# The first layer's start of a two-layer backbone: modulation, norm and first products in another order

## The chip, the cores and the metric

The kernel runs on one core of a Trainium2 chip. The metric is the time of one execution in microseconds (us) on the device. Five engines take their instructions in order, each from its own list, and wait for one another by semaphores: TensorE (PE, matrix products and transposes), VectorE (DVE), ScalarE (ACT), GpSimd (POOL) and SyncE (SP, which issues most loads).

## The reference

Two layers are run over 128 context tokens and 256 latent tokens (384 in all, of width 1024). What the change touches is the begin of layer 0:

```python
def rmsnorm(x, g):
    return x * rsqrt(mean(x * x, axis=-1) + EPS) * g
...
m = c @ w_ada + b_ada                      # shift, scale, gate of each of 1024 channels
h = rmsnorm(x, g1) * (1 + scale) + shift   # one set for context tokens, one for latent tokens
z = h @ w_in                               # split among four parallel groups:
# A neighbourhood attention, B a state-space (S5) block, C grouped-query attention, D latent attention
```

Group B is a diagonal complex recurrence. The kernel computes it by tables of powers of its complex decay factors (P), rotations (rw) and products of these with the input and output matrices B and C.

## The kernel before, in words

Activations stand transposed in SBUF, channels on the 128 partitions, 384 tokens along a row: x is eight such rows. Every matrix product of 32-bit numbers is done as three with rounded parts, high by high, low by high and high by low (L296, L297, L298). Each weight tile (`raw`) is therefore rounded by ScalarE (`hi`, L288), and VectorE subtracts to get the remainder (`lo`, L289); activations likewise have `ah` and `al`.

`first` (L1386 on) opens layer 0. It sums the squares of the eight rows of x (`prestat`), transposes the sums and makes the inverse norm (`inv_rms`). Then it goes over the eight rows k of 128 channels. `load(k)` issues on SyncE the two 512 KB tiles of modulation weights of the row, and every second row 512 KB of input weights; five modulation tiles fit at once (NA0). `mod(k)` is 16 matmuls (`pa`) and an eviction to `ar` on ScalarE. `norm(k)` transposes `ar` (L1428), reduces it on VectorE (L1431), adds the bias (`mods`, L1433), makes the gain (L1437), splits the weights, and for the context and the latent segment apart writes `ah` and `xn` on ScalarE (L1443, L1445) and `al` on VectorE (L1449). `products(k - LAG)` are the twelve matmuls of a row two rows back; `over_rms` (L1477) multiplies x by the inverse norm, five rows ahead of the loop and three after row 0.

Beside this VectorE computes group B's parameters: `fill(n)` takes n steps from a generator, first the parameters (`s5_params`, the s5t names; part of it on GpSimd: the powers P, and u and f), then the rotation `s5_rot` by doubling (`rw`, to 816 columns, L490 to L501) and the steps behind it. ScalarE copies the powers into the tables PQ and PF (L622 to L628) and the rotation into three buffers w (L662 on); a fourth, of magnitudes, is written by VectorE (L666). Four stores on GpSimd's queue (L672) write all to DRAM as `sw`. The buffers w stand in memory that the attention uses later (k4, v4, bias). Behind `first`, `tables0` (L1529) loads B, C and D and makes for each of four blocks of groups a table `eb` (512 columns, from PQ) and `ca` (640 columns, from PF); TensorE transposes `eb` (L707) and multiplies `ca` by the input factor (`ptr<-ca,bb`, L726).

The order of TensorE, ScalarE, VectorE and SyncE within `first` is that of the code, written by hand; GpSimd's and all that follows is ordered by a scheduler from priorities, and the mixer's parts by a list of steps.

Of the kernel before, what the change touches and what calls it, by code (L numbers as in the profile page):

```python
# [12 lines left out]
F32 = mybir.dt.float32  # L13
# [7 lines left out]
L = 2  # L21
# [17 lines left out]
NX = 5  # L39
FA = (4, 3, 4, 3, 4, 3, 4, 3)  # L40
FB = (8, 8, 4)
FK = ((0, 0, 0, 0, 0, 0), (1, 1, 1, 2, 2, 2), (1, 1, 1, 2, 2, 2), (1, 1, 1, 2, 2, 2), (1, 1, 1, 2, 2, 2), (1, 1, 1, 2, 2, 2), (1, 1, 1, 2, 2, 2), (1, 1, 1, 2, 2, 2))
FX = (6, 4, 4, 2, 2, 2, 2, 2)
MG = 0
WK = (0, 0, 0)
# [8 lines left out]
LAG = 2  # L54
# [74 lines left out]
def _prepare(a):  # L129
# [79 lines left out]
    r["cst"] = _constants()[0]  # L209
# [7 lines left out]
def _program(tc, I, O):  # L217
# [25 lines left out]
    def adjacent(calls):  # L243
# [6 lines left out]
    s5p = cp.tile([128, 5, 32], F32, name="s5p")  # L250
    A.dma_start(s5p, I["s5p"].rearrange("p (a b) -> p a b", a=5))
    csb = cp.tile([128, 8, 2], F32, name="csb")
    A.dma_start(csb, I["cT"].rearrange("p (k s) -> p k s", k=8))
    _, co = _constants()
    cst = cp.tile([128, int(co[-1])], F32, name="cst")
    A.dma_start(cst[:, :int(co[2])], I["cst"][:, :int(co[2])])
    ident, W1, W2, W4, RG, RM, cosg, sing, cosm, sinm, nadd = [
        cst[:, int(co[i]):int(co[i + 1])] for i in range(11)]
# [4 lines left out]
    vec = cp.tile([128, L * VPL], F32, name="vec")  # L263
    A.dma_start(vec[:, :VPL], I["vec"][:, :VPL])
# [3 lines left out]
    def vcol(l, i, n=1):  # L268
        return vec[:, l * VPL + i:l * VPL + i + n]
# [247 lines left out]

    def s5_params(qp, rest):
# [98 lines left out]
        G.tensor_tensor(f_[1], a[5], rden, op=OP.mult)  # L617
        yield

        def copies():  # L620
            for i, p in enumerate(P):
                A.activation(PQ[i][0:64], p[0:64, 0:8].rearrange("p t g -> p g t"), AF.Copy)  # L622
                yield
                A.activation(PQ[i][64:128], p[64:128, 7::-1].rearrange("p t g -> p g t"), AF.Copy)
                yield
                A.activation(PF[i][0:64, 0:9], p[0:64], AF.Copy)
                yield
                A.activation(PF[i][64:128, 1:10], p[64:128, ::-1], AF.Copy)  # L628
                yield
# [17 lines left out]
    def s5_rot(l, w, w4, qp, cmp):  # L647

        lg = slice(16 * l, 16 * l + 16)
        V.memset(w[0][:, :, 0:1], 1.0)  # L650
        V.memset(w[1][:, :, 0:1], 0.0)
        for i in range(2):
            V.tensor_copy(w[i][:, :, 1], u8[i][:, lg])
            yield
        h = 1
        while h < NC - 1:
            n = min(h, NC - 1 - h)
            shp = [128, 16, n]
# [3 lines left out]
        A.activation(w4[0], w[0], AF.Copy)  # L662
        A.activation(w4[1], w[1], AF.Copy)
        A.activation(w4[2], w[1], AF.Copy, scale=-1.0)
# [721 lines left out]
    def first(up, steps, rest):  # L1386
# [38 lines left out]
        def norm(k, ar, xb):  # L1425
            tr = pt()
            for q in range(2):
                PE.transpose(tr[:, 128 * q:128 * q + 128], ar[:, 128 * q:128 * q + 128], ident)  # L1428
            n = FK[k]
            m = tiny((2, 2))  # L1430
            V.tensor_reduce(m, tr[:, :256].rearrange("p (i c r) -> p i r c", i=2, c=4)[:, :, 0:2], axis=AX.X, op=OP.add)  # L1431
            fill(n[0])
            V.tensor_tensor(mods[0][:, k:k + 9:8], m,  # L1433
                            vcol(0, VO["adab"] + k, 9)[:, 0:9:8, None].to_broadcast([128, 2, 2]), op=OP.add)
            fill(n[1])
            Am = tiny((2,))
            V.tensor_scalar(Am, mods[0][:, 8 + k], 1.0, vcol(0, VO["n1"] + k), op0=OP.add, op1=OP.mult)  # L1437
            fill(n[2])
            W.append(split1(wr[k // 2], 512 * (k % 2), 512 * (k % 2) + 512))
            xn = kp.tile([128, XT[2]], F32, name="xn", tag=XT[0], bufs=XT[1])  # L1440
            hi, lo = act_pair()
            for s, (a, b) in enumerate(NSEG):
                A.activation(hi[:, a:b], xb[k // 2][:, k % 2, a:b], AF.Identity, scale=Am[:, s:s + 1],  # L1443
                             bias=mods[0][:, k, s:s + 1])
                A.activation(xn[:, a:b], xb[k // 2][:, k % 2, a:b], AF.Copy, scale=Am[:, s:s + 1])  # L1445
                late_a = nc.cur_bb.bb.instructions[-1]
            for s, (a, b) in enumerate(NSEG):
                fill(n[3 + s])
                V.scalar_tensor_tensor(lo[:, a:b], xn[:, a:b], mods[0][:, k, s:s + 1], hi[:, a:b].bitcast(F32),  # L1449
                                       op0=OP.add, op1=OP.subtract)  # L1450
            late = nc.cur_bb.bb.instructions[-1]
            fill(n[5])
            H.append((hi, lo))
            return late, late_a
# [19 lines left out]
        def over_rms(k):  # L1474
            if k % 2 == 0:
                xb.append(pools[1].tile([128, 2, T], F32, name="xb", tag="q3", bufs=NQ))
            V.tensor_tensor(xb[k // 2][:, k % 2], x[:, k], bc[:, :T], op=OP.mult)  # L1477

        for k in range(NX):
            over_rms(k)  # L1480
            fill(FX[k])
        for k in range(8 + LAG):
            if k < 6:
                load(k + 2)
            if k == 6:
                SY.dma_start(cst[:, int(co[2]):], I["cst"][:, int(co[2]):])
                SY.dma_start(vec[:, VPL:], I["vec"][:, VPL:])
            if 0 < k < 8:
                ars.append(mod(k))
            if k >= LAG:  # L1490
                products(k - LAG)
            if k < 8:
                late, late_a = norm(k, ars[k], xb)
            if k == 0:
                for i in range(NX, 8):
                    over_rms(i)
                    fill(FX[i])
                for _ in steps[0]:
                    pass
                steps[0] = itertools.chain(*rest)  # L1500
            for _ in range(WK[k] if k < LAG else 0):
                PE.matmul(zs[3][:, :T], warm[:, :128], warm, start=True, stop=True)
# [26 lines left out]
    def tables0():  # L1529
        bcd = s5_load(0, cmp)  # L1530
# [50 lines left out]
```

## Time and profile before

| | |
|---|---|
| median of 3 runs | 1104.14 us (1103.63 to 1106.66) |
| profiled run | 1105.24 us, span 1103.5 us, mean granted clock 0.987 |
| busy, TensorE | 1059.3 us, 96% of the span |
| busy, VectorE | 801.5 us, 73% |
| busy, ScalarE | 582.4 us, 53% |
| busy, GpSimd | 85.5 us, 8% |

The profile is of one execution. Busy time is a sum over the whole span; how full an engine is in one stage is seen from its busy time in that stretch. In rows of instructions the first number is the start in us from the span's start, the second the time that the row's instructions took.

### The profile page before, as it was taken

What the parts mean: (1) busy time and instruction counts of PE and PEld (TensorE: products, weight loads), DVE (VectorE), ACT (ScalarE), POOL (GpSimd) and SP (SyncE); (2) the same over time, 40 slices, a digit from 0 to 9 for tenths busy, and PEclk for the clock granted to TensorE, in tenths of its full rate; (3) what the DMA queues carried; (4) which work ended last, traced back from release to release, by engine and by line L of the source; (5) the groups of instructions that cost most, each with busy time, mean ns of one, the idle gap of its engine ahead of it and who ended that gap; (6) DMA issues with size and microseconds to landing.
All of it is one profiled execution on the core that took longest, in us unless ns stands there. A gap on an engine that the chain in (4) does not pass through costs nothing.

```text
span 1103.5 us, 18695 instructions
## 1 busy us (share of the span) xinstructions
PE 1059.3 (96%) x6724; PEld 904.8 (82%) x6724; DVE 801.5 (73%) x2026; ACT 582.4 (53%) x1251; POOL 85.5 (8%) x197
## 2 busy tenths in 40 slices
PE   6799988999999999999999999899999999999998
PEld 3577665447989999999999787545799999999998
DVE  6898677767899954679967787667669775476753
ACT  3754535455676543455457545564568553355532
POOL 4213111000100000001110220100000000000000
PEclk8999998999999999999999999999999999999999
DMA  8979866454554434445454874435333433433343
GB/s 331 320 260 304 246 207 225 156 179 172 172 178 134 140 106 139 131 134 163 129 158 157 218 233 137 129 125 183 116 115 96 138 114 117 148 126 123 116 131 98
DMA packets 64700, 182.19 MB, mean 165 GB/s; under 512 B 15840, under 2 KB 19168, under 8 KB 64608
## 3 DMA queue, kind: packets, MB, share of 16 engines
q1 hardware_dynamic: 55456, 152.52, 42.6%
q0 software_dynamic: 8576, 28.16, 8.3%
q8 instruction: 53, 0.87, 0.3%
q10 hardware_dynamic: 576, 0.32, 0.1%
q14 instruction: 39, 0.32, 0.1%
HBM read 166.19 MB, written 14.78 MB: 164 GB/s over the span
## 4 chain that ended last, share of the span: by engine, by line
PE 65%; DVE 4%; DMA 2%; ACT 1%; issue 0%; POOL 0%; SPq 0%; DVEq 0%; POOLq 0%; ACTq 0%
PE pz L296 11%; PE pz L297 10%; PE pz L298 10%; PE psc L298 8%; PE psc L297 8%; PE psc L296 8%; PE pa L319 2%; PE psc L959 1%; DVE lo L289 1%; DMA bias<-rpb 1%; PE ptr L963 1%; PE po L978 1%; DMA tbw<-sw 1%; PE psc L782 0%; DMA sw<-rw 0%
## 5 line engine op out<-in xcount | busy, mean ns | idle before, releaser
L288 ACT ACTIVATE hi<-raw 128x512 fp32r<-128x512 f32 (+2 forms) x396 | 228.1, 585 | 275.1 <-PE pz L297 109.1
L289 DVE TENSOR_TENSOR lo<-raw,hi 128x512 fp32r<-128x512 f32 (+2 forms) x396 | 250.2, 635 | 150.4 <-ACT hi L288 103.6
L296 PE MATMUL pz<-ah,hi 128*128 128x386 f32 (+1 forms) x616 | 213.8, 348 | 1.4 <-ACT gs L882 0.8
L297 PE MATMUL pz<-al,hi 128*128 128x386 f32 (+1 forms) x616 | 210.8, 343 | 1.0 <-DVE al L427 1.0
L298 PE MATMUL pz<-ah,lo 128*128 128x386 f32 (+1 forms) x616 | 210.2, 341 | 0.1
L296 PEld LDWEIGHTS pz<-ah,hi 128*128 128x128 f32 x616 | 116.5, 189 | 18.9 <-issue 13.4
L297 PEld LDWEIGHTS pz<-al,hi 128*128 128x128 f32 x616 | 117.0, 190 | 6.0 <-issue 3.6
L298 PEld LDWEIGHTS pz<-ah,lo 128*128 128x128 f32 x616 | 116.7, 190 | 3.0 <-issue 2.2
L296 PE MATMUL psc<-ah,hi 128*128 128x386 f32 (+1 forms) x336 | 114.2, 340 | 0.0
L298 PE MATMUL psc<-ah,lo 128*128 128x386 f32 (+1 forms) x336 | 113.9, 339 | 0.1
L297 PE MATMUL psc<-al,hi 128*128 128x386 f32 (+1 forms) x336 | 114.0, 339 | 0.0
L319 PE MATMUL pa<-raw,cw 128*32 128x256 f32 x640 | 62.5, 393 | 3.5 <-DMA raw<-ada 3.5
L296 PEld LDWEIGHTS psc<-ah,hi 128*128 128x128 f32 x336 | 63.5, 189 | 0.7 <-issue 0.4
L298 PEld LDWEIGHTS psc<-ah,lo 128*128 128x128 f32 x336 | 63.4, 189 | 0.4 <-DVE lo L289 0.4
L297 PEld LDWEIGHTS psc<-al,hi 128*128 128x128 f32 x336 | 63.7, 189 | 0.0
L296 PE MATMUL pz<-fh,hi 128*128 128x384 f32 x176 | 59.4, 338 | 0.1
L298 PE MATMUL pz<-fh,lo 128*128 128x384 f32 x176 | 59.5, 338 | 0.0
L297 PE MATMUL psc<-fl,hi 128*128 128x384 f32 x176 | 59.3, 337 | 0.0
L296 PE MATMUL psc<-fh,hi 128*128 128x384 f32 x176 | 59.3, 337 | 0.0
L297 PE MATMUL pz<-fl,hi 128*128 128x384 f32 x176 | 59.3, 337 | 0.0
L298 PE MATMUL psc<-fh,lo 128*128 128x384 f32 x176 | 59.3, 337 | 0.0
L936 ACT ACTIVATE P<-psc,ty 128x384 f32<-128x384 f32 (+1 forms) x56 | 32.2, 576 | 34.8 <-DVE ty L935 30.9
(431 smaller groups left out, 1950.3 us busy)
## 6 DMA issues: line engine op xcount, KB each, us to landing
raw<-wup SPq DMA_DIRECT2D x88, 512.0 KB, 3.5
raw<-ada SPq DMA_DIRECT2D x80, 512.0 KB, 4.6
raw<-win SPq DMA_DIRECT2D x30, 512.0 KB, 5.5
raw<-wdn SPq DMA_DIRECT2D x32, 384.0 KB, 3.1
raw<-wdn SPq DMA_DIRECT2D x32, 320.0 KB, 2.8
a<-ada SPq DMA_DIRECT2D x16, 512.0 KB, 6.1
raw<-wout SPq DMA_DIRECT2D x16, 512.0 KB, 3.5
se<-tbo POOLq DMA_DIRECT2D x16, 256.0 KB, 4.4
```

The lines of the kernel that those rows point to most:

```text
L288: A.activation(hi[:, :n], raw[:, a:b], AF.Copy)
L289: V.tensor_tensor(lo[:, :n], raw[:, a:b], hi[:, :n].bitcast(F32), op=OP.subtract)
L296: PE.matmul(out, wh, xh, start=start, stop=False)
L297: PE.matmul(out, wh, xl, start=False, stop=False)
L298: PE.matmul(out, wl, xh, start=False, stop=stop)
L319: PE.matmul(acc[32 * c:32 * c + 32, 256 * h:256 * h + 256], cw[:, kc], raw[:, 256 * c:256 * c + 256], start=kc == 0 and h == 0, stop=kc == ...
L936: A.activation(P[:, :w], S[:, :w], AF.Exp, bias=mx, scale=scale, accum_out=rs)
L959: PE.matmul(S[:, :T], qf(1 + qb), kf(128, 512), start=True, stop=True)
L963: PE.transpose(tr[:, 128 * kb:128 * kb + 128], P[:, 128 * kb:128 * kb + 128], ident)
L978: calls.append(lambda kb=kb, j=j: PE.matmul(o[64 * j:64 * j + 64, 128:T], heads[j][2](1 + kb), PTs[j][1][:, kb].rearrange("p q c -> p (q c ...
```

## The change

The loads of the state-space parameters, of c, of the first constants (the identity and a matrix of ones) and of layer 0's small vectors, four on ScalarE's queue, are one tensor `boot` with one load. The rest of the constants and layer 1's vectors are loaded at row 4, not at row 6. B, C and D of layer 0 are loaded behind the instruction that writes f (`mark`).

The rows are pipelined in another way. The transposes of row k+1 stand behind the products of row k-1 (one row back in place of two); the modulation runs two rows ahead, and its eviction stands ahead of the row's copies on ScalarE. Weights are rounded one row ahead. The inverse norm is copied from PSUM to SBUF once (`bcs`), and multiplied to x one row ahead. ScalarE writes the normed row in full precision (`y`, two segments) and then one rounded copy of 384 columns; VectorE subtracts them in one instruction. The fill steps per row (FK) are nine in six places before, and six (1, 1 and 4) in rows 2 to 7 after; what is left of the parameters comes behind row 0's remainder.

The eight copies into PQ and PF and, in layer 0, the three of the rotation go from ScalarE to GpSimd.

```diff
-FK = ((0, 0, 0, 0, 0, 0), (1, 1, 1, 2, 2, 2), ...)   # seven such rows
-FX = (6, 4, 4, 2, 2, 2, 2, 2)
+FK = ((0, 0, 0),) * 2 + ((1, 1, 4),) * 6
...
+    boot = cp.tile([128, nb + 160], F32, name="boot")
+    A.dma_start(boot, I["boot"])
...
         G.tensor_tensor(f_[1], a[5], rden, op=OP.mult)
+        mark.append(nc.cur_bb.bb.instructions[-1])
...
-                A.activation(PQ[i][0:64], p[0:64, 0:8].rearrange("p t g -> p g t"), AF.Copy)
+                G.tensor_copy(PQ[i][0:64], p[0:64, 0:8].rearrange("p t g -> p g t"))
...
+            G.tensor_copy(w4[0], w[0])
+            G.tensor_copy(w4[1], w[1])
+            G.tensor_scalar(w4[2], w[1], -1.0, None, op0=OP.mult)
...
+        def rows_hi(k, Am):
+            y = kp.tile([128, T], F32, name="y", tag="sq", bufs=5)
             hi, lo = act_pair()
             for s, (a, b) in enumerate(NSEG):
+                A.activation(y[:, a:b], xb[k // 2][:, k % 2, a:b], AF.Identity, scale=Am[:, s:s + 1],
                              bias=mods[0][:, k, s:s + 1])
+            A.activation(hi[:, :T], y[:, :T], AF.Copy)
...
+        def rows_lo(k, y):
+            V.tensor_tensor(lo[:, :T], y[:, :T], hi[:, :T].bitcast(F32), op=OP.subtract)
...
+        load(2)
+        tr = turned(0)
+        ars.append(mod(1))
+        weights_hi(0)
+        over_rms(0, bc)
+        for k in range(8):
+            if k + 3 < 8:
+                load(k + 3)
+            if k + 2 < 8:
+                ars.append(mod(k + 2))
+            Am = gain(k, tr)
+            y = rows_hi(k, Am)
+            if k == 0:
+                A.activation(bcs[:, :T], bc[:, :T], AF.Copy)
+            weights_lo(k)
+            if k < 7:
+                weights_hi(k + 1)
+                over_rms(k + 1, bcs)
+            rows_lo(k, y)
+            if k:
+                products(k - 1)
+            if k < 7:
+                tr = turned(k + 1)
+            if k == 0:
+                for _ in steps[0]:
+                    pass
+                steps[0] = itertools.chain(*rest)
+            fill(FK[k][2])
+        products(7)
...
+        with tc.issue_after(mark[0]):
+            bcd = s5_load(0, cmp)
```

VectorE at the first row of the pipeline, before (xb is the row times the inverse norm, the s5t names are set-up steps, `ty`, `mods` and `ty` the gain's three):

```order
L569 SCALAR_TENSOR_TENSOR s5t_149<-s5t_148,s5t_145 128x32
L1477 TENSOR_TENSOR xb<-x,ptr 128x384
L570 TENSOR_SCALAR s5t_150<-s5t_150 128x32
L545 TENSOR_TENSOR s5t_284<-s5t_149 128x32
L546 TENSOR_TENSOR s5t_285<-s5t_149,s5t_150 128x32
L547 TENSOR_SCALAR s5t_151<-s5t_284 128x32
L1477 TENSOR_TENSOR xb<-x,ptr 128x384
L548 TENSOR_TENSOR s5t_152<-s5t_285 128x32
L1477 TENSOR_TENSOR xb<-x,ptr 128x384 x2
L1431 TENSOR_REDUCE ty<-ptr 128x4
L1433 TENSOR_TENSOR mods_93<-ty,vec 128x2x2
L1437 TENSOR_SCALAR ty<-mods_93,vec 128x2
```

And the same place after:

```order
L1493 TENSOR_TENSOR xb<-x,ptr 128x384
L1439 TENSOR_REDUCE ty<-ptr 128x4
L1441 TENSOR_TENSOR mods_89<-ty,boot 128x2x2
L1445 TENSOR_SCALAR ty<-mods_89,boot 128x2
L1455 TENSOR_TENSOR lo<-raw,hi 128x512
L1493 TENSOR_TENSOR xb<-x,bcs 128x384
L1470 TENSOR_TENSOR al<-y,ah 128x384
L542 SCALAR_TENSOR_TENSOR s5t_146<-s5t_146,s5t_143 128x32
L542 SCALAR_TENSOR_TENSOR s5t_144<-s5t_144,s5t_143 128x32
```

The gain now stands behind one xb; the set-up steps have moved behind the row's remainder `al`.

GpSimd behind the powers P, before: it issues the stores of the rotation, then those of the tables.

```order
L501 TENSOR_TENSOR P_293<-cm_357,cm_358 128x128
L672 DMA sw_108<-w_433 512x1x204
L672 DMA sw_108<-w_434 512x1x204
L672 DMA sw_108<-w_435 512x1x204
L672 DMA sw_108<-w_436 512x1x204
L711 DMA se_104<-tbo 128x512 x2
```

And after:

```order
L625 COPY PQ_94<-P_343 64x256
L626 COPY PQ_94<-P_343 64x256
L627 COPY PF_92<-P_343 64x288
L628 COPY PF_92<-P_343 64x288
L667 COPY w_495<-rw 128x816
L677 DMA sw_104<-w_498 512x1x204
L668 COPY w_496<-rw 128x816
L669 TENSOR_SCALAR w_497<-rw 128x816
L677 DMA sw_104<-w_495 512x1x204
L677 DMA sw_104<-w_496 512x1x204
L677 DMA sw_104<-w_497 512x1x204
L716 DMA se_100<-tbo 128x512 x2
```

The copies stand in the list, and three of the four stores behind the last of them.

ScalarE, with its waits, where it evicts the neighbourhood keys (`nkT`), before:

```order
L288 ACTIVATE hi<-raw 128x512 [waits DMAHW3_49,DVE_49,PE_49]
L900 ACTIVATE sq<-pz 128x384 [waits PE_49]
L1028 ACTIVATE nkT<-pz,vec 128x384 [waits DMASW3_49]
L288 ACTIVATE hi<-raw 128x512 [waits DVE_49]
L731 ACTIVATE KT<-ptr 128x112 [waits DMAHW6_49,DMAHW5_49,DMAHW7_49,DMAHW0_49,PE_49]
```

And after:

```order
L288 ACTIVATE hi<-raw 128x512 [waits DVE_49,PE_49]
L905 ACTIVATE sq<-pz 128x384 [waits PE_49]
L1033 ACTIVATE nkT<-pz,boot 128x384 [waits DMASW4_49,Pool_49]
L288 ACTIVATE hi<-raw 128x512 [waits DMAHW4_49,DVE_49,PE_49]
L715 ACTIVATE tbo<-ptr 128x512 [waits PE_49]
```

The eviction waits for a store from GpSimd's queue in both, and now for GpSimd itself too; the table's evictions have moved behind it.

## Rows read from the trace of the kernel before

**Rows 1.** Stretches: length, busy PE, PEld, DVE, ACT, POOL (count), clock, DMA share, GB/s

```profile
0.00:20.00 20.00, 11.63 (x66) 4.97 (x66) 13.53 (x79) 6.43 (x12) 5.27 (x25) 1.00 0.92 351
20.00:40.00 20.00, 16.88 (x120) 11.98 (x120) 16.76 (x64) 11.72 (x29) 11.10 (x36) 0.83 0.79 293
40.00:60.00 20.00, 14.25 (x100) 9.65 (x103) 16.25 (x53) 15.86 (x33) 3.27 (x4) 0.91 0.91 290
60.00:80.00 20.00, 19.79 (x198) 16.94 (x192) 19.27 (x31) 10.13 (x22) 3.99 (x7) 1.00 0.87 312
80.00:100.00 20.00, 17.89 (x166) 14.44 (x152) 19.48 (x30) 7.77 (x17) 5.61 (x6) 0.91 0.86 284
```

**Rows 2.** Timeline, TensorE, rows stage: start, us, shapes, in brackets the wait before

```profile
9.07 0.85 PE L392 MATMUL po<-sq,cst 128*32 128x384 f32 x8 [1.65 <-DMA cst<-cst]
...
13.66 1.07 PE L1419 MATMUL pa<-a,cw 128*32 128x256 f32 x16
...
32.48 0.44 PE L1428 MATMUL ptr<-cst,ar 128*128 128x128 f32 x2 [0.24 <-ACT ar L1422]
...
36.06 0.38 PE L1428 MATMUL ptr<-cst,ar 128*128 128x128 f32 x2
...
59.45 0.45 PE L296 MATMUL pz<-ah,hi 128*128 128x384 f32 x1 [0.50 <-ACT ah L1443]
```

**Rows 3.** Timeline, ScalarE, row copies, a rotation copy and the eviction of the keys

```profile
19.91 0.49 ACT L1443 ACTIVATE ah<-xb,mods,ty 128x128 fp32r<-128x128 f32 x1 [4.21 <-DVE ty L1437]
...
30.48 0.50 ACT L1443 ACTIVATE ah<-xb,mods,ty 128x128 fp32r<-128x128 f32 x1 [1.49 <-DVE ty L1437]
...
41.55 0.89 ACT L662 ACTIVATE w<-rw 128x816 f32<-128x816 f32 x1 [1.54 <-DVE rw L494]
...
68.41 0.57 ACT L1028 ACTIVATE nkT<-pz,vec 128x384 f32<-128x384 f32 x1
```

**Rows 4.** Timeline, GpSimd: power chain's ends, a store's issue, an addition later

```profile
17.83 0.25 POOL L604 TENSOR_TENSOR P<-s5t,s5t 128x32 f32<-128x32 f32 x1 [1.55 <-DVE s5t L547]
...
25.33 0.21 POOL L596 COPY u<-s5t 128x32 f32<-128x32 f32 x1
...
42.73 1.12 POOL L672 DMA_DIRECT2D sw<-w  x1 [10.98 <-ACT w L662]
...
84.74 2.53 POOL L1150 TENSOR_TENSOR bias<-bias,cst 128x1024 f32<-128x1024 f32 x1 [4.17 <-DMA raw<-win]
```

**Rows 5.** Timeline, VectorE: the rotation's first copy, one table product at two places

```profile
25.57 0.18 DVE L653 COPY rw<-u 128x16 f32<-128x16 f32 x1 [1.93 <-POOL u L596]
...
63.02 0.82 DVE L493 TENSOR_TENSOR cm<-PF,s5bc 128x640 f32<-128x640 f32 x1
...
84.94 3.02 DVE L493 TENSOR_TENSOR cm<-PF,s5bc 128x640 f32<-128x640 f32 x1
```

**Rows 6.** Groups by shape, VectorE, 24 to 60 us: count, busy us, mean ns, idle

```profile
L494 DVE TENSOR_TENSOR eb<-cm,cm 128x512 f32<-128x512 f32 x1 | 0.7, 694 | 0.0
...
L681 DVE TENSOR_TENSOR a<-s5p,sel 128x16 f32<-128x16 f32 x4 | 0.6, 168 | 0.0
L666 DVE COPY w<-rho 128x816 f32<-128x816 f32 x1 | 0.6, 582 | 0.0
...
L494 DVE TENSOR_TENSOR rw<-cm,cm 128x288 f32<-128x288 f32 x1 | 0.4, 449 | 0.0
```

**Rows 7.** Timeline, TensorE behind the tables: last table products, and three waits

```profile
105.90 0.67 PE L726 MATMUL ptr<-ca,bb 64*32 64x128 f32 x32
...
111.65 0.55 PE L917 MATMUL ptr<-cst,stz 128*128 128x128 f32 x3 [0.53 <-ACT stz L913]
...
114.78 0.64 PE L319 MATMUL pa<-raw,cw 128*32 128x256 f32 x8 [1.19 <-DMA raw<-ada]
...
151.63 0.59 PE L959 MATMUL psc<-nkT,nqT 64*128 64x384 f32 x1 [3.31 <-ACT P L930]
```

**Rows 8.** The stores of the rotation: from issue to landing

```profile
DMA to landing us min/median/max: 7.5/8.5/9.0
```

More of the change, by code (lines that the diff above doesn't have):

```diff
@@ L208, in _prepare @@
     r["wglu"] = np.stack([pk(a["s5_w_glu"][l]) for l in range(L)])
[L209 removed]
+    cst, co = _constants()
+    r["cst"] = cst[:, co[2]:]
+    vec = r.pop("vec")
+    r["boot"] = np.concatenate([r.pop("cT"), cst[:, :co[2]], vec[:, :VPL], r.pop("s5p")], 1)
+    r["vec1"] = vec[:, VPL:]
     return {n: np.ascontiguousarray(v, dtype=f) for n, v in r.items()}
@@ L248, in adjacent @@
                 c()
[L250 to L253, printed above, removed]
     _, co = _constants()
[L255 to L258, printed above, removed]
+    co = [int(i) for i in co]
+    nb = 16 + co[2] + VPL
+    boot = cp.tile([128, nb + 160], F32, name="boot")
+    A.dma_start(boot, I["boot"])
+    csb = boot[:, 0:16].rearrange("p (k s) -> p k s", k=8)
+    s5p = boot[:, nb:].rearrange("p (a b) -> p a b", a=5)
+    cst = cp.tile([128, co[-1] - co[2]], F32, name="cst")
+    ident, W1 = [boot[:, 16 + co[i]:16 + co[i + 1]] for i in range(2)]
+    W2, W4, RG, RM, cosg, sing, cosm, sinm, nadd = [cst[:, co[i] - co[2]:co[i + 1] - co[2]] for i in range(2, 11)]
     x = cp.tile([128, 8, T], F32, name="x")
@@ L1423, in mod, with turned, gain @@
             return ar
-        def norm(k, ar, xb):
+        def turned(k):
             tr = pt()
             for q in range(2):
-                PE.transpose(tr[:, 128 * q:128 * q + 128], ar[:, 128 * q:128 * q + 128], ident)
-            n = FK[k]
+                PE.transpose(tr[:, 128 * q:128 * q + 128], ars[k][:, 128 * q:128 * q + 128], ident)
+            return tr
+        def gain(k, tr):
             m = tiny((2, 2))
             V.tensor_reduce(m, tr[:, :256].rearrange("p (i c r) -> p i r c", i=2, c=4)[:, :, 0:2], axis=AX.X, op=OP.add)
-            fill(n[0])
+            fill(FK[k][0])
@@ new lines, in weights_hi, with weights_lo @@
+        def weights_hi(k):
+            hi = wp.tile([128, 512], F32R, name="hi", tag="hi", bufs=NHI)
+            A.activation(hi, wr[k // 2][:, 512 * (k % 2):512 * (k % 2) + 512], AF.Copy)
+            W.append([hi])
+        def weights_lo(k):
+            lo = wp.tile([128, 512], F32R, name="lo", tag="lo", bufs=NLO)
+            V.tensor_tensor(lo, wr[k // 2][:, 512 * (k % 2):512 * (k % 2) + 512], W[k][0].bitcast(F32), op=OP.subtract)
+            W[k].append(lo)
+        def rows_hi(k, Am):
+            y = kp.tile([128, T], F32, name="y", tag="sq", bufs=5)
@@ L1447, in norm @@
[L1447 to L1452, printed above, removed]
+            A.activation(hi[:, :T], y[:, :T], AF.Copy)
             H.append((hi, lo))
-            return late, late_a
+            return y
+        def rows_lo(k, y):
+            hi, lo = H[k]
+            V.tensor_tensor(lo[:, :T], y[:, :T], hi[:, :T].bitcast(F32), op=OP.subtract)
@@ L1472, in first, with over_rms @@
         xb = []
-        def over_rms(k):
+        def over_rms(k, r):
             if k % 2 == 0:
                 xb.append(pools[1].tile([128, 2, T], F32, name="xb", tag="q3", bufs=NQ))
[L1477 to L1493, printed above, removed]
-            if k == 0:
-                for i in range(NX, 8):
-                    over_rms(i)
-                    fill(FX[i])
+            V.tensor_tensor(xb[k // 2][:, k % 2], x[:, k], r[:, :T], op=OP.mult)
+        load(2)
[3 more added lines that the diff above has]
+        over_rms(0, bc)
+        bcs = pools[2].tile([128, 512], F32, name="bcs", tag="rp", bufs=1)
+        for k in range(8):
+            if k + 3 < 8:
+                load(k + 3)
+            if k == 4:
+                SY.dma_start(cst, I["cst"])
+                SY.dma_start(vec[1], I["vec1"])
+            if k + 2 < 8:
+                ars.append(mod(k + 2))
+            Am = gain(k, tr)
+            y = rows_hi(k, Am)
+            late_a = nc.cur_bb.bb.instructions[-1]
+            if k == 0:
+                A.activation(bcs[:, :T], bc[:, :T], AF.Copy)
[4 more added lines that the diff above has]
+            rows_lo(k, y)
+            late = nc.cur_bb.bb.instructions[-1]
+            if k:
[3 more added lines that the diff above has]
+            if k == 0:
                 for _ in steps[0]:
```

39 lines of the change are left out of this document (13 added, 26 removed).

## The prediction

> **What bounds the kernel now.** I read the busy times in stretches of 20 us first, since the change touches only the first layer's start. TensorE has work for 16.88 of the 20 us from 20 to 40 and for 14.25 of those from 40 to 60, but for 19.79 from 60 to 80 [rows 1]. So there is slack for TensorE only while the first products are made. From 60 to 100 VectorE is as full as TensorE (19.27 and 19.48 of 20) [rows 1]: there it computes the tables of the state-space group, and every such table is wanted by TensorE before it may go on to the next part. A gain ahead of 60 us is thus kept only if VectorE's tables come earlier too, or if TensorE has other work in hand.
>
> Then the rows of instructions on TensorE. Its first products stood still 1.65 us for the constants [rows 2]; from the first modulation at 13.66 to the last row's products at 59.45 eight rows took 45.8 us, though one unhindered round, from the transposes at 32.48 to those at 36.06, took 3.58 [rows 2]. What is late is the chain transposes, VectorE's gain, ScalarE's copies, VectorE's remainder: the first row's copy on ScalarE waited 4.21 us for VectorE's gain, the third's 1.49 [rows 3], since VectorE held set-up steps ahead of the gains and 63 fill steps between them.
>
> **The start.** One load in place of four lets the statistics begin without the wait for the constants; the wider load is itself no shorter, so of 1.65 us [rows 2] I take 1.2 (0 to 1.65). In the order after, the first gain stands directly behind one row's product with the inverse norm; the eleven set-up steps that stood ahead of it are behind the row's remainder. With the modulation at some 12.5, and the one of row 2 now ahead of row 0's copies on ScalarE, these start at about 17.9 against 19.91 [rows 3]: two us early. The early gain does not last to row 2. GpSimd computes from 17.83 to 25.33 what the rotation's first copies read, and VectorE waited 1.93 us for it at 25.57 [rows 4, 5]. Those copies still stand ahead of row 2's gain. GpSimd's inputs come from the set-up steps, which end at about 22.2 (four us later than before), and its chain lasts 7.5 us [rows 4] with the moved loads' issue in it (some 0.7), so the copies are done near 30.4 and row 2's copy on ScalarE starts at about 31.0, as before (30.48) [rows 3]. The loads of B, C and D, moved behind that chain, have over 20 us till their first reader, which hides them.
>
> **Rows 3 to 7.** A row now costs VectorE three small steps, a weight remainder, one norm product and one subtraction of 384 columns in place of two, and six fill steps in a block. The fills grow from 16 to 256 columns, so the rounds are some 3.6 (TensorE's own round [rows 2]) for two rows, then 4.1 and 4.9. On top lies what GpSimd does to VectorE, which the trace does show: a product of 640 columns took 3.02 us at 84.94, while GpSimd's addition of 84.74 ran for 2.53, against 0.82 at 63.02 [rows 4, 5]. The eight table copies of 256 and 288 columns, in this stretch, can therefore cost VectorE from 1.5 us (a third of them met) to 5.5 (all). The last row's remainder then ends at 54 (51.5 to 57) and TensorE's last products of the stage start some 5.5 us before 59.45 [rows 2] (2.5 to 8).
>
> In the Trainium skill, "SBUF — State Buffer", section "Who interferes with whom", a VectorE instruction with two SBUF inputs and a GpSimd instruction that reads SBUF exclude each other, and whichever began first keeps the port until it ends; the row of 3.02 us agrees with it. By that rule the whole of each GpSimd copy is lost to such a VectorE step, which is the upper end above; it speaks against this part of the change.
>
> **What VectorE owes at that point.** 36 fill steps replace 63. When row 7's remainder is done before, VectorE has also done these, which after it has still to do: six 288-wide rotation products (0.45 each, 2.7), the copy of the 816-wide magnitudes and four selections (1.4), their six products (1.0), the six of the input factor (256 columns, a little under the 288, 2.5), and half of the first table (three of 0.69, 2.1) [rows 6]; 9.7 us in all. None of it has gone away; it has moved behind the pipeline. Against the 5.5 us won that is a loss of 4.2 at the tables.
>
> **The copies on GpSimd, and a new wait.** ScalarE loses eight copies and three of 816 columns (0.89 each [rows 3]); ScalarE is not the bound there (11.72 and 15.86 us busy of 20 in rows 1), so that itself is worth nothing. GpSimd has no copy that wide in the trace. Bounds: its copy of 32 columns took 0.21 us and its addition of 1024 took 2.53 [rows 4]; scaled by columns between these the 816-wide copy takes from 1.15 (half of the addition's rate, one input instead of two) to 2.2; I take 1.8, nearer to the wide row. In the order after, all four stores of the rotation stand behind or among the copies: the stores of the copied tables follow the third copy. Rotation done at 3.9 us behind the last remainder (the rotation products and the steps between them), two further copies, an issue of 1.12 [rows 4] and a landing of 7.5 to 9.0 as before [rows 8] put the store's end some 14.4 to 18.4 us after the remainder (3.9, 2.3, 0.7 and 7.5; or 3.9, 4.4, 1.1 and 9.0). ScalarE's eviction of the neighbourhood keys, at 68.41 before and then without a wait [rows 3], writes into the buffer of the first copy and so waits for that store; behind it stand the rounding of the next weights and, on VectorE, their remainder, and TensorE's next products behind these. VectorE would reach that remainder 11.5 to 15.5 us after. A stall of 2.5 us (0 to 5).
>
> In the Trainium skill, "GPSIMD Engine Reference", section "3.1 Elementwise — side-by-side cycle accounting", an element costs GpSimd some 2.6 cycles and VectorE one; no run here shows such a copy, and by that figure an estimate is 1.77 us for 816 columns, which would leave the sum as it stands.
>
> **The sum.** Before, the last group's products of the tables start on TensorE at 105.90 [rows 7], 46.4 us after the last row's products at 59.45 [rows 2]. After: 54 and 46.4, and 9.7 owed, and 2.5 of stall, is 112.6: 6.7 us late (2 to 12). TensorE has done other work meanwhile: in the order after, the next steps of the list (the context's norm and the next modulation) are taken ahead of this place, worth some 4 us less to do behind it. That would leave 2.7 us of loss; since part of that other work reads what VectorE also makes later, and VectorE has only 0.5 us of idle from 80 to 100 [rows 1] to catch up, I carry 4. Three waits that follow then find their data older: 0.53 for the standardised context, 1.19 for a weight load [rows 7], which are gone but for some 0.5 of new ones, and 3.31 at 151.63 [rows 7] for the neighbourhood bias, which TensorE reaches later by the loss while the bias comes from a load that does not move; it falls to about 1. So minus 1.2 and minus 2.3. In all 4.0 less 3.5: **0.5 us slower**. Everything behind that is the same list on every engine. The profiled run took 1105.24 us with a span of 1103.5; the median is 1.1 under this run, so I add to the median: 1104.14 and 0.5, or 1104.6.
>
> **The rivals.** First, **the pipeline's gain is kept**: the wide copies take 1.15 us, the copies meet VectorE rarely (1.5), the last remainder is done at 51.5 and the store lands before VectorE gets there, so there is no stall. Then the tables end at 51.5, 46.4 and 9.7, or 107.6, 1.7 late, of which the 4 us of other work make a gain of 2.3; with the 1.2 of the waits and up to 2.5 of the bias it is 6 us: 1098. For it: TensorE's own round of 3.58 and 45.8 us for eight of them. Against: 3.02 in place of 0.82.
>
> Second, **GpSimd becomes the clock of the tables**: the copies take 2.2 us each, the narrow ones hit VectorE in full (5.5), the last remainder is at 57, the stall is 5. Tables at 57, 46.4, 9.7 and 5 would be 118, less the 4 of work, 8 late, less the 3.5 of waits, and one more of these from 111 on not gained: 1109 to 1110. It decides from about 1.8 us a wide copy on, where the store lands later than VectorE arrives. For it: 2.53 us for 1024 columns; against: that is an addition of two inputs.
>
> Third, **the loads set the pace**, so that nothing moves in the rows: the DMA engines are at 0.92 and 0.79 of their time up to 40 us [rows 1]. But with 351 and 293 GB/s [rows 1] the 10.5 MB of the rows (eight of 1 MB, and the first weights) are there at about 33 to 40 us, and the last row is read past 50; I exclude it as a limit and give it no chance of its own.
>
> **How the numbers follow.** A measurement here tells 0.3%, 3.3 us, from no change: 1100.8 to 1107.5 is the same. The forecast, a head start that the tables eat up, has 0.41; the first rival 0.32, the second 0.27; these are also the chances of same, faster and slower. The range reaches 7 or 8 us to the first side, with the lock cheap and the bias wait gone, and 6 us to the other: 1097 to 1110.5.
>
> **What would show it.** Right steps: TensorE's statistics begin without a wait for constants; the first ScalarE copy of a row at about 18; VectorE waiting for GpSimd ahead of row 2; the last row's products at 54; GpSimd's wide copies at 1.8 us with VectorE steps of 1 to 2 us beside them; ScalarE's eviction waiting for a store; the last tables' products at 112; the wait for the bias near 1 us. Wrong: the last products at 51 or under and no wait at the eviction (then the first rival), the wait at the eviction over 4 us (the second), or any difference behind 180 us, where the lists are the same.

## The result, and the profile after

The changed kernel takes 1119.08 us (median; 1116.98 to 1121.34) against 1104.39 for the kernel before beside it: 14.7 us slower, ratio 1.0130 with an interval of 1.0105 to 1.0155. Run again later (e9) the ratio was 1.0143 (1.0121 to 1.0164). Hardly any change was forecast (1104.6), with 1110.5 as the upper end of the range: the forecast was wrong, and the time lies 8.6 us above that end. Now and then an execution is disturbed and takes hundreds of us longer; the times below leave such executions out, and the profile of e3, which fell in one, is not read.

The page of the profiled execution (span 1119.5) opens with:

```profile
span 1119.5 us, 18682 instructions
PE 1066.7 (95%) x6724; PEld 909.2 (81%) x6724; DVE 802.5 (72%) x2018; ACT 575.6 (51%) x1233; POOL 94.5 (8%) x208
```

The stretches of 20 us of the kernel after, columns as in [rows 1]:

```profile
0.00:20.00 20.00, 12.96 (x84) 5.50 (x84) 10.82 (x64) 8.11 (x16) 1.50 (x13) 0.98 0.91 348
20.00:40.00 20.00, 16.11 (x107) 11.06 (x108) 11.88 (x44) 8.42 (x18) 16.35 (x49) 0.77 1.00 383
40.00:60.00 20.00, 17.82 (x119) 13.24 (x120) 19.01 (x58) 11.47 (x24) 5.55 (x9) 1.00 0.48 174
60.00:80.00 20.00, 17.38 (x124) 15.90 (x131) 17.64 (x37) 7.35 (x15) 7.28 (x9) 0.91 0.89 280
80.00:100.00 20.00, 14.43 (x150) 11.16 (x151) 13.94 (x23) 6.68 (x14) 5.32 (x5) 0.86 0.87 282
```

Against [rows 1] TensorE does more up to 60 us and much less from 60 to 100 (17.38 and 14.43 against 19.79 and 17.89). TensorE's timeline, in the columns of [rows 2], shows the places: the last row's products (56.34), the first table (69.91), the first and the last group's products of the tables (79.86 and 120.55), between them a wait for a load of weights (96.45), and the norm behind them (122.26, its transposes 128.01).

```profile
56.34 0.45 PE L296 MATMUL pz<-ah,hi 128*128 128x384 f32 x1 [0.43 <-ACT ah L1464]
...
69.91 0.70 PE L712 MATMUL ptr<-boot,eb 128*128 128x128 f32 x4 [2.25 <-DVE eb L494]
...
79.86 0.67 PE L731 MATMUL ptr<-ca,bb 64*32 64x128 f32 x32
...
96.45 1.08 PE L319 MATMUL pa<-raw,cw 128*32 128x256 f32 x8 [5.26 <-DMA raw<-ada]
...
120.55 1.11 PE L731 MATMUL ptr<-ca,bb 64*32 64x128 f32 x32
122.26 1.51 PE L912 MATMUL ptr<-sq,cst 128*32 128x384 f32 x8 [0.60 <-DVE KT L738]
...
128.01 0.66 PE L922 MATMUL ptr<-boot,stz 128*128 128x128 f32 x3
```

The last products come 3.1 us earlier than in [rows 2], the last tables' products 14.65 us later than in [rows 7], the norm's transposes 16.4 us later (128.01 against 111.65), and the span is 16.0 us longer. All of the loss lies between 57 and 128 us; behind that the lists are the same and so is the time.

VectorE's idle time has this size. Its busy time (the third pair of numbers) up to the norm's products, of the kernel before:

```profile
0.00:40.00 40.00, 28.52 (x186) 16.95 (x186) 30.28 (x142) 18.15 (x40) 16.37 (x60) 0.91 0.86 322
40.00:60.00 20.00, 14.25 (x100) 9.65 (x103) 16.25 (x53) 15.86 (x33) 3.27 (x4) 0.91 0.91 290
60.00:107.00 47.00, 44.68 (x418) 37.93 (x413) 43.91 (x68) 20.63 (x45) 11.04 (x14) 0.96 0.88 303
```

and after:

```profile
0.00:40.00 40.00, 29.07 (x191) 16.57 (x192) 22.70 (x108) 16.53 (x33) 17.85 (x62) 0.87 0.95 365
40.00:60.00 20.00, 17.82 (x119) 13.24 (x120) 19.01 (x58) 11.47 (x24) 5.55 (x9) 1.00 0.48 174
60.00:122.00 62.00, 48.70 (x444) 38.87 (x443) 49.64 (x88) 19.82 (x43) 16.59 (x20) 0.89 0.86 283
```

The work is the same, 90.4 us in 107 and 91.4 us in 122. What differs is idle time: 9.7 against 17.3 us in the first 40, 3.8 against 1.0 from 40 to 60, 3.1 against 12.4 behind. The sums, 16.6 and 30.7, differ by 14 us, of which 4.8 lie in the first 60 us and 9.3 behind. VectorE's waits up to 60 us, after (wait, us in all, times, longest):

```profile
DVE rw L653 <- POOL u L598: 4.7, 1, 4.7
DVE sq L387 <- DMA x<-xT: 3.8, 2, 3.5
DVE xb L1493 <- ACT bcs L1513: 3.2, 1, 3.2
```

The first was 1.9 us before; the third is new. Behind 57 us VectorE waits for ScalarE's rounding of weights, and ScalarE for weights and a store:

```profile
DVE lo L289 <- ACT hi L288: 8.1, 3, 5.8
```

```profile
ACT hi L288 <- DMA raw<-win: 7.8, 3, 5.9
ACT nkT L1033 <- DMA sw<-w: 5.8, 1, 5.8
```

The places on ScalarE and VectorE, then SyncE's waits for the rotation's stores and its issue of the weights that came late:

```profile
70.57 0.58 ACT L1033 ACTIVATE nkT<-pz,boot 128x384 f32<-128x384 f32 x1 [5.79 <-DMA sw<-w]
...
91.59 1.29 DVE L289 TENSOR_TENSOR lo<-raw,hi 128x512 fp32r<-128x512 f32 x2 [5.80 <-ACT hi L288]
```

```profile
SPq L1056 <- DMA sw<-w: 5.2, 1, 5.2
...
SPq L1073 <- DMA sw<-w: 2.5, 1, 2.5
```

```profile
77.88 3.63 SPq L276 DMA_DIRECT2D raw<-win  x2
```

In the kernel before the same two loads were issued from 73.65 on. Ahead of them SyncE had stood 5.2 and 2.5 us for the rotation's stores, the first time until 70.54; before, its wait for them was over at 50.32.

### The profile page after: what moved, and what is told of

The parts are those of the page before. It is cut to its first block, busy times and chain, and to the rows that moved or that the text cites. A ratio compares the mean times of both kernels' runs of the same rounds, so it can differ in the third digit from the quotient of the medians.

```text
span 1119.5 us, 18682 instructions
## 1 busy us (share of the span) xinstructions
PE 1066.7 (95%) x6724; PEld 909.2 (81%) x6724; DVE 802.5 (72%) x2018; ACT 575.6 (51%) x1233; POOL 94.5 (8%) x208
## 4 chain that ended last, share of the span: by engine, by line
PE 64%; DVE 4%; DMA 2%; ACT 1%; issue 1%; POOL 0%; SPq 0%; DVEq 0%; POOLq 0%; ACTq 0%
PE pz L296 10%; PE pz L297 10%; PE pz L298 10%; PE psc L298 8%; PE psc L297 8%; PE psc L296 8%; PE pa L319 2%; PE psc L964 1%; DVE lo L289 1%; DMA bias<-rpb 1%; PE ptr L968 1%; PE po L983 1%; DMA tbw<-sw 1%; DMA sw<-rw 0%; PE psc L787 0%
## 5 line engine op out<-in xcount | busy, mean ns | idle before, releaser
L288 ACT ACTIVATE hi<-raw 128x512 fp32r<-128x512 f32 (+2 forms) x388 | 222.8, 584 | 276.2 <-PE pz L297 107.5
L289 DVE TENSOR_TENSOR lo<-raw,hi 128x512 fp32r<-128x512 f32 (+2 forms) x388 | 244.5, 633 | 149.9 <-ACT hi L288 106.2
```

Of the source, the lines that this page charges most:

```text
L288: A.activation(hi[:, :n], raw[:, a:b], AF.Copy)
L289: V.tensor_tensor(lo[:, :n], raw[:, a:b], hi[:, :n].bitcast(F32), op=OP.subtract)
```

## The experiments

Two theories were set against each other. Theory A: the copies on GpSimd, and the stores that wait for them, cost the time. Theory B: VectorE stands idle in the rows and owes the tables' steps behind them. A third, theory C, was the order of loads on SyncE. Each ratio is to the kernel before on the same chip, with its 95% interval in brackets. e1 to e8, e9 to e12 and e13 to e18 ran on three chips; across these groups only the ratios are compared.

**e1**, the three wide copies back on ScalarE:

```diff
-        if l:
-            A.activation(w4[0], w[0], AF.Copy)
...
-        else:
-            G.tensor_copy(w4[0], w[0])
...
+        A.activation(w4[0], w[0], AF.Copy)
```

> The changed kernel, with the three 816-wide copies of the rotation back on ScalarE; nothing else. Against the changed kernel's 1119.1 us. Theory A (GpSimd's copies and the stores behind them are the loss): the third copy took GpSimd 2.25 us and all are done at 64.2; on ScalarE at 0.89 each they are done near 63, the store lands 1.5 to 2.5 us earlier and the wait of 5.8 us before the keys' eviction shrinks by as much: 1114 to 1117. Theory B (VectorE's table steps, moved behind the rows, are the loss): 1118 to 1120, and ScalarE's copies stand in front of its evictions.

Measured: 1119.93 us, 1.0115 [1.0064, 1.0165]. Nothing that can be told from the changed kernel, though in its profile the keys' eviction waited 2.60 us in place of 5.79.

**e2**, more fill steps per row:

```diff
-FK = ((0, 0, 0),) * 2 + ((1, 1, 4),) * 6
+FK = ((0, 0, 0),) * 2 + ((1, 1, 7),) * 6
```

> The changed kernel with nine fill steps in each of rows 2 to 7 in place of six: 54 in place of 36, so that the rotation, the magnitudes and the selections are done within the rows. Theory B: 18 steps of 0.2 to 0.45 us, some 7 us, leave the place behind the rows; the rows have slack for about half of that, the last products begin at 58 to 60 in place of 56.3, and the tables end 5 to 9 us earlier: 1109 to 1114. Theory A: the stores start as much earlier, so that the wait at the keys goes too, and nothing tells the two apart but that wait: were it all, 1113 (5.8 less). Theory C (weight loads held up behind loads of modulation weights that wait for TensorE): the DMA engines stay idle from 44 to 51 and the time falls by under 3.

Measured: 1116.78 us, 1.0083 [1.0053, 1.0114], about 5 us less than the changed kernel by the ratios: the low end of B. The way was not the one that was expected: the last row's products began at 65.84 (expected 58 to 60), and the last tables' products at 120.04, only 0.5 us earlier.

**e3**, two stores straight from the rotation's buffers:

```diff
-            G.tensor_copy(w4[0], w[0])
-            G.tensor_copy(w4[1], w[1])
...
+            wi = w[i] if i < 2 and not l else w4[i]
```

> The changed kernel with the first two stores of the rotation made straight from the rotation's own buffers, without the two copies; the third copy stays on GpSimd. No store then reads the keys' buffers, and the eviction of the keys waits for none. Theory A: the 5.8 us of wait at the eviction and the 5.2 us that SyncE waits for the store both go: 1111 to 1114. Theory B: the tables of VectorE are as late as before (last ones at 120), and the time falls by 2 us at most: 1117 to 1119.

Measured: 1120.93 us, 1.0130 [1.0087, 1.0173], from three executions. No gain, against A.

**e4**, the kernel before with only the copies moved to GpSimd (the edit is the change's own):

> The kernel before, with the eight table copies and the three of the rotation on GpSimd and nothing else of the change. Against 1104.4 us. Theory A: 3 to 8 us slower, by a later store and by VectorE steps that run beside the copies. Theory B: within 2 us, since the steps of VectorE stand where they stood.

Measured: 1107.50 us, 1.0005 [0.9977, 1.0033]. No cost of the copies can be told there, where the rotation is done within the rows.

**e5**, no copies, and stores from x:

```diff
-            G.tensor_copy(w4[0], w[0])
-            G.tensor_copy(w4[1], w[1])
-            G.tensor_scalar(w4[2], w[1], -1.0, None, op0=OP.mult)
...
+            src = (w4[i] if l or i == 3 else x.rearrange("p k t -> p (k t)")[:, 816 * i:816 * i + 816]
+                   .rearrange("p (g m) -> p g m", g=16))
```

> The changed kernel without the three rotation copies, their stores made from x in place of the copies (what they hold is then wrong, and only the size of the traffic is kept). No store reads the keys', the values' or GpSimd's copy buffers, so neither ScalarE's eviction nor SyncE's loads of the cached keys and values wait for one. VectorE's list is kept. Theory A (the late stores, through ScalarE and SyncE, are the loss): 8 to 13 us less than the changed kernel, 1107 to 1111 beside a kernel before of 1105 to 1107. Theory B (VectorE's displaced table steps): 0 to 3 us less, 1117 to 1120.

Measured: 1118.65 us, 1.0094 [1.0052, 1.0136], overlapping the changed kernel's interval. By the ratios that is 4 to 5 us less, but it does not bound A. The three stores from x left at 8.1 to 9.6 us, among the rows' first loads, which the changed kernel's did not, and the last row's products came at 60.80, 4.5 us later than in the changed kernel. From there to the norm's products at 119.55 it took 58.8 us in place of 65.9, and VectorE's long waits for the rounding are gone. So A's share of the loss stays open, between nothing (e3) and some 7 us.

**e6**, the rotation left out:

```diff
-        while h < NC - 1:
+        while l and h < NC - 1:
...
```

> The changed kernel with layer 0's rotation products left out (36 steps of VectorE, 24 of them in the rows, the widest behind them; its buffers are filled by GpSimd at the start, so what follows from them is wrong). The copies and stores stay, but start early. VectorE has 2.7 us less behind the rows and up to 9 us less in them. Theory B: the tables come 5 to 8 us earlier and the time falls by 6 to 12: 1107 to 1113. Theory A gives the same by another way (stores early); the run before this one tells them apart. If neither holds, over 1116.

Measured: 1106.86 us, 0.9984 [0.9961, 1.0007]: level with the kernel before. Leaving out these steps takes away the whole loss. By itself this does not part the theories, since the stores are early here too.

**e7**, the set-up steps first:

```diff
+        for _ in steps[0]:
+            pass
+        steps[0] = itertools.chain(*rest)
         over_rms(0, bc)
...
-            if k == 0:
-                for _ in steps[0]:
-                    pass
-                steps[0] = itertools.chain(*rest)
             fill(FK[k][2])
```

> The changed kernel with the last eleven set-up steps ahead of row 0's gain again, as in the kernel before; the rest as changed. GpSimd starts its chain at about 16.5 in place of 23.0, the rotation's first values are there at 25 in place of 31.5, and VectorE's wait of 4.7 us ahead of row 2's gain goes; row 0 is 1.3 us later. The last products start at about 53 in place of 56.3. Theory B: the tables come as much earlier, 3 us, 1115 to 1117; if a lead in the rows is worth nothing, 1118 to 1120.

Measured: 1117.18 us, 1.0081 [1.0052, 1.0110]. By the ratios this is 5 to 7 us less than the changed kernel. VectorE's wait of 4.7 us is gone, and both the last row's products and the norm's transposes come some 4 us earlier than in the changed kernel, so this lead was kept:

```profile
52.11 0.44 PE L296 MATMUL pz<-ah,hi 128*128 128x384 f32 x1 [0.23 <-ACT ah L1464]
...
124.00 0.84 PE L922 MATMUL ptr<-boot,stz 128*128 128x128 f32 x3
```

Against the kernel before the rows led by 7.3 us, and the kernel was still 9 us slower: how early the rows end does not say how early the tables do.

**e8**, the merged load and the late loads of B, C and D in the kernel before:

> The kernel before with the merged first load and the late loads of B, C and D alone; rows, fills and copies as before, and the lists behind the start as before. 0 to 2 us less than the kernel before by all theories (1.65 us of wait gone at the start, of which VectorE's set-up may keep part); over 2 us more would mean that the late loads or the wider first one cost something.

Measured: 1105.95 us, 0.9992 [0.9961, 1.0022]: no effect that can be told, so the merged load and the late loads are not the loss.

**e9**, the changed kernel again, beside e10 to e12 on their chip: 1122.77 us, 1.0143 [1.0121, 1.0164].

> The changed kernel once more, unaltered, beside the three that follow on the same chip, since chips differ by a few us here: 1.3% over the kernel before, the last products at about 56 us, the fourth block's products of the tables some 14 us later than before.

**e10**, the first block's tables left out:

```diff
+            if not l and not b:
+                G.memset(eb, 0.5)
+            else:
               cmul([eb[:, 0], eb[:, 1]], ...
```

> The changed kernel without the first block's tables on VectorE: six products of 512 and six of 640 columns, 9 us, left out and their buffers filled by GpSimd (so the state-space block's result is wrong). The rotation, its copies and its stores stay as late as they are. Theory B alone (VectorE has too much behind the rows): the time falls by 7 to 12 us, to the kernel before. Theory A alone (the late stores): 0 to 2 us. Both in turn: 3 to 6.

Measured: 1113.05 us, 1.0043 [1.0024, 1.0062]: 9.7 us less than e9, though the wide copies, and so the stores behind them, came 3.5 us later than in the changed kernel (the first at 62.28 against 58.78). Nine us of VectorE's work for ten of the kernel's time is B, and hardly A. Its VectorE is busy 22.59, 15.82 and 45.08 us in the three stretches:

```profile
0.00:40.00 40.00, 29.04 (x190) 16.46 (x190) 22.59 (x107) 16.53 (x33) 17.67 (x62) 0.87 0.95 362
40.00:60.00 20.00, 17.77 (x114) 12.26 (x110) 15.82 (x49) 10.24 (x21) 8.15 (x12) 0.91 0.40 141
60.00:120.00 60.00, 49.48 (x449) 41.13 (x450) 45.08 (x86) 23.15 (x51) 19.02 (x23) 0.94 0.83 282
```

**e11**, e2 and e7 together:

> The changed kernel with the eleven set-up steps ahead of row 0's gain and nine fill steps per row in rows 2 to 7 in place of six. Under theory B both edits fill time in which VectorE was idle (4.7 us at row 2, some 3 in the rows) with work that it did behind them: 5 to 9 us less than the changed kernel. If only the lead of the rows counted, the added fills would cost as much as they bring: 1115 to 1118.

Measured: 1113.24 us, 1.0057 [1.0032, 1.0082]: 9.5 us less than e9, with nothing left out. VectorE is busy 27.09 us in the first 40, against 22.70. The rows ended late, the last products 4.9 us behind the changed kernel's and 1.8 behind those of the kernel before:

```profile
61.20 0.69 PE L296 MATMUL pz<-ah,hi 128*128 128x384 f32 x1 [2.05 <-ACT ah L1464]
```

So VectorE's early work counts, and not the end of the rows. The stores are early as well (the last copy ends at 55.3, not 64.2, and the keys' eviction does not wait), so e11 alone does not part A from B.

**e12**, e11 with the tables later in the mixer's list:

```diff
-'AATGTATAGGGTTTTGTATAGGGNGAG...
+'AAGAGATAGTGTGTTGTATGTGTNGAG...
```

> The same as the run before, and the mixer's list of steps asks for the tables' steps later among the input products (the same steps, nine table steps spread over the first 24 places). If TensorE, which takes its list in order, loses its time by standing at products whose tables are not ready, 2 to 5 us less than the run before; if VectorE's total of work up to the last table is all that counts, no change.

Measured: 1112.38 us, 1.0049 [1.0030, 1.0067], which can't be told from e11.

**e13**, e11 with all copies on ScalarE:

> The run with set-up first and 54 fills, and all eleven copies back on ScalarE. With VectorE's idle time filled, what GpSimd's copies cost VectorE and the stores is seen by itself. Theory A: 2 to 5 us less than that run (1113.2 beside a kernel before of 1108.1, so 1.0057 becomes 1.001 to 1.004). Theory B: within 1.5 us of it.

Measured: 1114.76 us, 1.0101 [1.0079, 1.0123]. No gain on e11 (1.0057), if anything a loss: against A. VectorE there waits 8.4 us behind the rows for ScalarE's rounding, 4.2 in e11; whether the copies stood in ScalarE's way was not shown.

**e14**, e11 with e5's stores:

> The run with set-up first and 54 fills, its rotation stored from x without copies (what is stored is wrong, the traffic the same), so that nothing waits for those stores. If the late stores are the rest of the loss, 4 to 6 us less, level with the kernel before; if not, within 2 us of the ratio 1.0057.

Measured: 1112.28 us, 1.0074 [1.0047, 1.0101]: no gain that can be told. The waits for the stores are not what is left, as far as the stores from x, early as in e5, allow to say so.

**e15**, e11 with two buffers for ca:

```diff
-            ca = qp.tile([128, 2, 4, 10, 16], F32, name="ca", tag="ca", bufs=1)
+            ca = qp.tile([128, 2, 4, 10, 16], F32, name="ca", tag="ca", bufs=2 - l)
```

> The run with set-up first and 54 fills, and two buffers for the table ca of layer 0. In that run VectorE waited 4.3 us at 86.5 for the store of the first ca, which shared the DMA engines with four small-packet loads of the bias; with two buffers that wait goes. If VectorE's list is the bound, 3 to 5 us less, ratio 1.001 to 1.003; if the loads of weights are, no change.

Measured: 1110.36 us, 1.0046 [1.0023, 1.0068], not told from e11, though its wait is gone. VectorE's waits of e11 from 50 to 118 us:

```profile
DVE ca L494 <- DMA sf<-ca: 4.3, 1, 4.3
DVE lo L289 <- ACT hi L288: 4.2, 8, 1.0
```

and of e15:

```profile
DVE lo L289 <- ACT hi L288: 3.0, 3, 1.4
```

**e16**, e15 and e12 together:

> As the run before it, and the table steps later in the mixer's list. A try for the best time: 0 to 3 us less than that run, and at best 3 us under the kernel before, since the rows lead by some 5 us and VectorE has the same tables to make.

Measured: 1107.04 us, 1.0022 [0.9998, 1.0046]: not told from the kernel before, and the best version of the change that leaves nothing out.

**e17**, the kernel before with fewer fill steps, nothing of the change in it:

```diff
-FK = ((0, 0, 0, 0, 0, 0), (1, 1, 1, 2, 2, 2), ...)
+FK = ((0, 0, 0, 0, 0, 0),) + ((1, 1, 0, 1, 1, 0),) * 7
```

> The kernel before, with four fill steps per row in rows 1 to 7 in place of nine (28 in place of 63) and nothing else: rows, copies, loads and first load as before. The steps left out of the rows come behind them, as in the changed kernel. Theory B: VectorE then stands idle in the rows, owes about 10 us behind them, and the kernel is 6 to 12 us slower than before, though the rows end some us earlier. If the loss belongs to the new pipeline, its copies or its loads, it is within 3 us of the kernel before.

Measured: 1116.75 us, 1.0110 [1.0074, 1.0145]. The rows end earlier than in the kernel before and the norm's transposes come 12.7 us later, as in the changed kernel:

```profile
54.68 0.45 PE L296 MATMUL pz<-ah,hi 128*128 128x384 f32 x1 [1.67 <-ACT hi L288]
...
93.27 0.77 PE L726 MATMUL ptr<-ca,bb 64*32 64x128 f32 x32 [4.77 <-DVE ca L499]
...
124.34 0.84 PE L917 MATMUL ptr<-cst,stz 128*128 128x128 f32 x3
```

This is the change's loss without the change: cutting the fill alone makes a kernel 12 us slower by the ratio. By what way, it does not say. VectorE's stretches up to 60 us, and its two longest waits from 55 to 118 us:

```profile
0.00:40.00 40.00, 28.53 (x204) 17.01 (x204) 27.41 (x132) 18.78 (x41) 16.34 (x60) 0.91 0.87 326
40.00:60.00 20.00, 18.33 (x125) 14.50 (x118) 17.20 (x60) 16.71 (x35) 2.95 (x4) 0.91 0.78 281
```

```profile
DVE lo L289 <- ACT hi L288: 5.6, 5, 2.4
DVE ca L494 <- DMA sf<-ca: 5.0, 1, 5.0
```

At 60 us VectorE has done only 1.9 us less than in the kernel before; the rest of its additional idle time lies behind the rows, in waits such as these. The rotation's stores are late here too, because the rotation is: SyncE's load that waits for the first of them went out at 63.66, against 50.32 before and 70.54 in the changed kernel.

**e18**, e16 with row 1's norm product from PSUM:

```diff
-                over_rms(k + 1, bcs)
+                over_rms(k + 1, bcs if k else bc)
```

> The best version so far (set-up first, 54 fills, two buffers for ca, table steps later), and row 1's product with the inverse norm taken from PSUM, so that VectorE doesn't wait 3.2 us for ScalarE's copy at row 0. Theory B: up to 1 us less than that version (1.0022), since VectorE's next step waits for ScalarE too.

Measured: 1110.26 us, 1.0039 [1.0021, 1.0057]: no gain over e16. No version was faster than the kernel before by more than the noise.

## Why the prediction was wrong, step by step

**What bounds.** Right: a lead ahead of 60 us is kept only if the tables come earlier: in e17 the rows led by 4.8 us and the kernel lost 12, in e7 4 us of lead came through to the norm. VectorE is the engine on which that hangs (e10, e11, e17).

**The start.** Right in kind: TensorE's statistics start at 7.76 with no wait for constants. Row 0's copies on ScalarE began at 18.86, forecast 17.9. At row 2 the forecast was level with before (31.0); it was 32.62. GpSimd's chain began at 23.0, not 22.2, and came to the copy of u at 31.5, 8.5 us later where it had been 7.5; 0.75 of that is the issue of a load inside it, which the forecast had. VectorE's 3.2 us for the copy of the inverse norm were not in it.

**The rows.** The last row's products at 56.34 lie in the range (51.5 to 57), 2.3 behind the forecast.

**The copies.** Wide ones took 0.87 and 0.86 us, not the 1.8 of the sum or the 1.77 that stood beside it, and the negating one 2.25. GpSimd after, then VectorE beside it:

```profile
58.78 0.87 POOL L667 COPY w<-rw 128x816 f32<-128x816 f32 x1 [14.17 <-DVE rw L494]
...
61.15 0.86 POOL L668 COPY w<-rw 128x816 f32<-128x816 f32 x1 [0.81 <-DVE sel L680]
61.98 2.25 POOL L669 TENSOR_SCALAR w<-rw 128x816 f32<-128x816 f32 x1
```

```profile
58.90 1.05 DVE L496 TENSOR_TENSOR cm<-rw 128x288 f32<-128x288 f32 x1
...
62.07 0.80 DVE L686 TENSOR_TENSOR a<-boot,sel 128x16 f32<-128x16 f32 x1
62.80 0.41 DVE L492 TENSOR_TENSOR cm<-f,s5bc 128x256 f32<-128x256 f32 x1
```

Steps of 0.45 and 0.17 us took 1.05 and 0.80, so VectorE does pay; but the step of 0.80 ended at 62.87, and the product at 62.80 took its usual 0.41 (0.42 before), while the negation ran on to 64.2. The Trainium skill ("SBUF — State Buffer", "Who interferes with whom") would have the lock held for all of GpSimd's instruction: the first row agrees, the other two do not. The second rival, GpSimd as the clock of the tables, came nearest in time (1110), and the sign named for it, a wait of over 4 us at the eviction, came true. By its mechanism it fell: the wide copies took half of its 2.2 us or less, and without them on GpSimd nothing was won (e1, e13).

**The new wait.** It came: ScalarE's eviction of the keys waited 5.79 us, until 70.57, 13.5 us after the last remainder's end at 57.05 (forecast 14.4 to 18.4). On VectorE it cost 1.94 us (forecast 2.5). Taking the wait at the keys away gave nothing (e3); what the stores cost through SyncE is open (e5).

**The sum.** Here the prediction failed, in two terms. The first is the stall. The tables were forecast at 112.6 and came at 120.55. Of the 7.95 us, 2.3 are the later rows (products at 56.34 for 54), and 5.2 are waits on VectorE that the sum had at 2.5 and that came to 7.7: the 1.94 through the store, and 5.80 at 91.59 for weights that were loaded late, a wait that the sum did not have. The 9.7 us owed were right in kind: the steps behind the last remainder are those that the forecast lists.

The second is the credit, which was to make 0.5 us of the 6.7 at the tables; in place of that 14.65 us became 16.0. TensorE had in fact done six pieces of the next modulation more, of eight matmuls each, when it came to the norm's products (16 against 10, 0.53 us each, 3.2 us). But none of the 4 us, of which the forecast counted 2.7, came back. Before, three pieces stood between the norm's products and its transposes; now none was left, and TensorE waited there for ScalarE. The granted clock from 120 to 140 us, behind TensorE's stops, was 0.79 where it had been 1.00:

```profile
125.28 0.69 PE L296 MATMUL pz<-ah,hi 128*128 128x384 f32 x1 [1.51 <-ACT XK L1031]
```

```profile
120.00:140.00 20.00, 17.23 (x110) 12.10 (x107) 9.00 (x32) 8.02 (x17) 8.03 (x14) 0.79 0.56 160
```

Nor did the waits that were to shrink give 3.5 us: the one of 1.19 for weights came as 1.76 and 0.56, and the one of 3.31 at 151.63 as 2.35 at 167.45. With no credit, the forecast's own tables would have been 6.7 us late. The size of that one term, 9.7 owed against a lead of 5.5, was the message: e17 shows that cutting the fill is enough for a loss of this size.

**What stays open.** That fewer fill steps in the rows cost the time is shown (e17, e11); by which way is in part open. From e11 to the kernel before are 5 to 6 us. The copies (e13), the stores (e14) and the store of ca (e15) are not these one by one; later tables and a second ca together (e16) leave 2.4 us that can't be told from nothing. How much of VectorE's 9.3 us more of idle time behind the rows follows from the late table steps, and how much from loads that wait for the buffers these steps free, was not parted; the stores reach these loads too, through SyncE. Of theory C only the first and the late loads were tried (e8); the order of the weight loads was not varied by itself.

## What to carry to other kernels

Where an engine is nearly full in one stage, its idle time in the stage ahead is the place where that work has to be done: count the engine's busy time up to the end of the second stage, not the speed of the first. Removing filler from a pipeline speeds the pipeline and hands the filler to the stage that can't take it; in e17 that cost more than VectorE's lag of 1.9 us at 60 us, by the waits that followed. A wait seen in a trace after a change is not yet its cause: here a new one of 5.79 us, at the keys, could be taken away without a gain (e3).

## What the runs showed of the hardware

A GpSimd copy of 128x816 in SBUF took 0.87 us, no longer than ScalarE's 0.89 [rows 3], but the same size with a multiplication 2.25. In e11, with wide VectorE steps beside them, the two copies took 1.09 and 1.27 and the multiplication 2.55. A chain of GpSimd steps that had run 7.5 us took 8.5 with one load's issue of 0.75 in it. Two 512 KB loads of input weights, issued behind the 128 KB loads of the bias, landed 12.9 and 13.0 us later (12.2 in the kernel before), where the median of such loads over the execution is 5.4; what held them was not tested. A TensorE that stood still 5.26 us ran behind it at a granted clock of 0.50, the lower of its two levels, from 95 to 100 us:

```profile
95.00:100.00 5.00, 3.55 (x37) 2.31 (x45) 4.87 (x8) 0.46 (x1) 0.91 (x1) 0.50 0.99 378
```
